# Banded attention blocks on 192 keys: a shared middle of 128 keys and two corners of 64 in a two-layer trunk on one core

## The chip, the core and the metric

One core of one Trainium2 chip runs the whole program; nothing is shared with another core. The metric is device time in microseconds (us) from start to end of one execution, lower is better. Five engines each take their own instructions in order: PE (TensorE, matrix products into PSUM; its weight loads are listed as PEld), DVE (VectorE), ACT (ScalarE), POOL (GpSimd) and SP (SyncE, which here only issues DMAs). They meet through semaphores.

## What is computed

Two layers with a residual stream of 1024 tokens by 1024 channels, all float32. The first is a gated short convolution, the second a dilated sliding-window attention with three groups of 16 heads of 64. Cut to what matters here:

```python
DILATED_GROUPS = ((128, 1), (512, 4), (2048, 16))
...
    proj = h @ w_in
    b_gate, c_gate, u, z = jnp.split(proj, 4, axis=-1)
    v = c_gate * u
    conv = sum(w_conv[k] * vp[:, k:k + S] for k in range(CONV_K))
    y = b_gate * conv * jax.nn.silu(z)
...
    logits = jnp.einsum('brhnqd,brhnkd->brhnqk', qs, kb).astype(jnp.float32) * (HEAD_DIM ** -0.5)
    step = BLOCK + a - kk
    valid = (step >= 0) & (step <= span) & (key_pos >= 0)
    logits = jnp.where(valid, logits + bias, -jnp.inf)
    probs = jnp.exp(logits - lse[..., None])
    out = jnp.einsum('brhnqk,brhnkd->brhnqd', probs.astype(v.dtype), vb)
```

In all three groups the window is 128 steps of the dilated sequence. A block of 128 queries therefore sees its own 128 keys and the 128 before them; the query at place a of the block needs the 129 keys from place a of the earlier block to place a of its own. The first 64 queries never need the second 64 keys of their own block, and the last 64 queries never need the first 64 keys of the earlier one: each half needs 192 of the 256. In group 0 the sequence is whole (8 blocks), in group 1 it falls into 4 residue classes (2 blocks each), in group 2 into 16 classes of 64 tokens, which have no earlier block.

## The kernel before

**Four stages.** The convolution's input products (up to some 630 us), its output products (to some 815 us), the attention's projections (to some 1590 us), and the attention itself with the output projection. The large products are split into high and low parts of type fp32r, three matmuls of 512 columns for each product; from pair to pair of weight blocks they go by Strassen's scheme (7 products of 12 matmuls in place of 8). `pair` and `strassen` (L310, L430) do that. At the start of the first stage, however, the channel blocks 0 and 1 are done plainly (L421: four weights, two halves each, 24 matmuls a product), while `mixed` (L190) prepares the sums of blocks of x (`T`) that Strassen's scheme needs, a quarter at each `next(mix)`.

**Attention.** A unit is one pair of heads (hp, 8 of them) and one group (g, 3). Its work is cut into steps: 4 for g = 0 and g = 1 with two blocks each, 2 for g = 2; 80 steps in all. `make` (L895) returns the parts of a step:

- A (L899): scores. q against k of both heads (s = 0 on partitions 0 to 63, s = 1 on 64 to 127) into a PSUM bank for each head. A block with an earlier block is here called wide, one without is called alone. A wide block takes four matmuls of 64 queries by 192 keys (L929), an alone one two of 128 by 128 (L924). DVE then adds the bias tile `bt`, negates, and takes the row's minimum (L942) into `xs`.
- E (L946): ACT's exponential of `xs` with the row's sum (L948).
- B (L950): PE transposes `xs` in pieces of 128 by 128 (L955) into a PSUM tile `pt`, and `copy` (L863) moves it to `pts`: for s = 0 on DVE in the first 22 steps (afterwards in every second step), otherwise on ACT.
- C (L959): the second product, values as weights against `pts`, into a PSUM tile `po` of 64 values by 512 queries for each head, one tile for each half of the sequence. `finish` (L983) copies a half to SBUF as soon as its last block is done. The 64 columns of one block's values stand 8 floats apart in the tile `V` (`[P, P, 8]`, key by value by block).

A wide block has two pieces of 128 keys in B and C, an alone one has one.

**What sets the order.** All five engines follow the order in which the program is written in this stage. The loop at L1228 runs over iterations k; in each it first emits A of step k, then C of step k-4 (`LC`), later pieces of older units (scaling, gate, splits), then B of step k-2 (`LB`), then E of step k, and in the end six matmuls of the output projection (`dense`, L1145) from iteration 36 on. SP loads q and k six steps ahead, the bias tiles with them, and V two steps ahead of a unit (its C comes four steps after its A). PSUM: three banks for scores, two for `pt`, two for `po`, one for `pd` of the output projection.

Of the kernel before, what the change touches and what calls it, by code (L numbers as in the profile page):

```python
# [19 lines left out]
P = 128  # L20
# [15 lines left out]
def trunk(ctx: ExitStack, tc: tile.TileContext, a, out):  # L36
# [92 lines left out]
    with tc.tile_pool(name="wq", bufs=1) as wq, tc.tile_pool(name="sle", bufs=1) as sle, \  # L129
# [199 lines left out]
        with tc.tile_pool(name="rp", bufs=1, side="right") as rp, tc.tile_pool(name="cp", bufs=2, side="right") as cp, \  # L329
# [490 lines left out]
    with tc.tile_pool(name="sp", bufs=1, space=PSUM) as sp, tc.tile_pool(name="ptp", bufs=2, space=PSUM) as ptp, \  # L820
# [11 lines left out]
        QK, VS, SZ, y2, part, ml = {}, {}, {}, {}, {}, {}  # L832
# [37 lines left out]
        def attention(hp, g):  # L870
# [4 lines left out]
            def prefetch():  # L875
                bt = []
                sk, w = ((sk0, 384), (sk1, 384), (sk2, 256))[g]
                for s in range(2):
# [5 lines left out]
                    else:  # L884
                        nc.sync.dma_start(b0, rows[:, :256])
# [9 lines left out]
            def make(js, first):  # L895

                c, xs, pts, exps = [], [], [], []

                def A():  # L899
# [6 lines left out]
                    for n, j in enumerate(js) if g == 2 else ():  # L906
# [6 lines left out]
                        if n % 2 == 0:  # L913
                            c.append((n // 2, j, 2 * j, True, True))
                    for n, j in enumerate(js) if g < 2 else ():
                        alone = j == 0 if g == 0 else j < 4
                        x0, nk = 2 * n, 1 if alone else 2
                        b = 2 * (j % 4) + j // 4 if g == 1 else j
                        vb = [b] if alone else [b - 1, b]
                        kv = slice(vb[0] * P, (b + 1) * P)  # L920
                        for s, hs in enumerate((lo, up)):
                            out_ = ps[s][:, x0:x0 + nk].rearrange("p a b -> p (a b)")
                            if alone:
                                nc.tensor.matmul(out_, q[hs, b * P:(b + 1) * P], k[hs, kv], start=True, stop=True)  # L924
                        if not alone:

                            for h in range(2):
                                for s, hs in enumerate((lo, up)):
                                    nc.tensor.matmul(ps[s][64 * h:64 * h + 64, x0:x0 + 2].rearrange("p a b -> p (a b)")  # L929
                                                     [:, 64 * h:64 * h + 192],  # L930
                                                     q[hs, b * P + 64 * h:b * P + 64 * h + 64],
                                                     k[hs, kv.start + 64 * h:kv.start + 64 * h + 192],
                                                     start=True, stop=True)
                        todo.append((slice(x0 * P, (x0 + nk) * P), j, slice(0 if nk == 2 else 128, 256)))
                        c.extend((x0 + i, j, vb[i], i == 0, i == nk - 1) for i in range(nk))
                    for s in range(2):
                        xs.append(ap.tile([P, 4, P], F32, name="xs", tag="xs", bufs=6))
# [11 lines left out]

                def B():  # L950
                    n = len(c)
                    for s in range(2):
                        pt = ptp.tile([P, 4, P], F32, name="pt", tag="pt")
                        for i in range(n):
                            nc.tensor.transpose(pt[:, i], xs[s][:, c[i][0]], ident)  # L955
                        pts.append(ap.tile([P, 4, P], F32, name="pts", tag="pts", bufs=6))
                        copy(pts[s][:, :n], pt[:, :n], s)

                def C():  # L959
                    for q in ((0, 1) if g == 2 else (js[0] // 4,)):  # L960
                        if js[0] == 0 or (g < 2 and js[0] == 4):
                            u["po", q] = opp.tile([P, HALF], F32, name="po", tag="po")
                    V = VS[hp, g]
                    for i, (x, j, vb, f, l) in enumerate(c):
                        for a in range(2) if g == 2 else ():
# [372 lines left out]
```

## Time and profile before

| | |
|---|---|
| median of 3 runs | 1924.93 us (1924.89 to 1928.53) |
| the profiled execution | 1926.97 us, its span 1925.2 us |
| PE busy over the span | 1893.9 us (98%), 10702 matmul records |
| DVE, ACT, POOL busy | 1480.2, 878.4, 901.0 us |
| HBM read and written | 192.53 and 67.64 MB |

The span is what the profiler saw of one execution; 1.8 us of the execution lie outside it. A matmul's record carries the partitions of its weights by their columns (`64*64`), then weights' and output's form. A float32 matmul leaves two records, a float32 transpose one, an fp32r matmul one. Matmuls on different parts of the array run beside each other, so the sum of their durations is more than the time they take; what a group takes is read from the starts in the timeline.

### The profile page before, as it was taken

How to read it: one execution, taken by the hardware profiler on the slowest of the kernel's cores; microseconds unless marked ns; L12 is line 12 of the kernel's file. 1: busy time of each engine (PE TensorE's matmuls, PEld its weight loads, DVE VectorE, ACT ScalarE, POOL GpSimd, SP SyncE). 2: the span in 40 equal slices, each digit the busy share in tenths (PEclk: the TensorE clock that was granted, in tenths of full speed). 3: DMA queues.
4: the chain of work that ended last, by engine and by line, in shares of the span. 5: the costliest groups of instructions: out<-in, count | busy, mean ns of one | idle time of the engine just before them, and what ended most of it. 6: DMA issues, size and time to landing. Idle time of an engine off the chain costs nothing.

```text
span 1925.2 us, 30180 instructions
## 1 busy us (share of the span) xinstructions
PE 1893.9 (98%) x10702; PEld 1549.7 (80%) x10702; DVE 1480.2 (77%) x2798; ACT 878.4 (46%) x2007; POOL 901.0 (47%) x835
## 2 busy tenths in 40 slices
PE   8999999999999999999999999999999998989999
PEld 6888888888888788888888888888888887767777
DVE  6966666666666746698898689869888877988896
ACT  6433333333333534454334443443344428867780
POOL 0356676766666211334545554555454551433240
PEclk9999999999999999999999999999999999989999
DMA  5312223222222656423323332333233338897842
GB/s 192 125 63 80 99 72 109 86 90 83 87 82 84 229 179 220 154 83 131 110 104 110 115 110 97 117 115 110 92 106 118 102 131 274 261 275 220 235 134 88
DMA packets 117800, 253.78 MB, mean 132 GB/s; under 512 B 18494, under 2 KB 23838, under 8 KB 117648
## 3 DMA queue, kind: packets, MB, share of 16 engines
q1 hardware_dynamic: 93280, 176.89, 28.4%
q0 software_dynamic: 24368, 74.95, 12.3%
q8 instruction: 84, 1.38, 0.3%
q14 instruction: 68, 0.56, 0.1%
HBM read 192.53 MB, written 67.64 MB: 135 GB/s over the span
## 4 chain that ended last, share of the span: by engine, by line
PE 89%; DMA 4%; DVE 3%; issue 2%; POOL 1%; ACT 1%; SPq 0%; DVEq 0%; POOLq 0%; ACTq 0%
PE pp L295 22%; PE pp L297 21%; PE pp L298 21%; PE pp L547 3%; PE pp L548 3%; PE pp L546 3%; PE po L976 2%; DMA nld<-nl 2%; PE pt L955 2%; PE pp L368 1%; PE pp L369 1%; PE pp L370 1%; PE ps L929 1%; PE pd L1150 1%; PE pd L1152 1%
## 5 line engine op out<-in xcount | busy, mean ns | idle before, releaser
L159 DVE TENSOR_TENSOR ws<-wr,ws 128x512 fp32r<-128x512 f32 x284 | 293.6, 1035 | 115.9 <-ACT ws L158 114.3
L158 ACT ACTIVATE ws<-wr 128x512 fp32r<-128x512 f32 x284 | 178.3, 630 | 368.3 <-PE pp L298 244.3
L158 ACT ACTIVATE ws<-sr 128x512 fp32r<-128x512 f32 x272 | 171.0, 631 | 349.6 <-PE pp L298 292.2
L159 DVE TENSOR_TENSOR ws<-sr,ws 128x512 fp32r<-128x512 f32 x272 | 226.4, 838 | 82.7 <-ACT ws L158 80.7
L270 POOL TENSOR_TENSOR sr<-wr 128x512 f32<-128x512 f32 x136 | 192.2, 1413 | 198.7 <-DMA wr<-in_conv_w_in 66.5
L307 DVE TENSOR_TENSOR f<-pp,f 128x512 f32<-128x512 f32 x204 | 139.6, 684 | 88.5 <-PE pp L298 81.3
L948 ACT ACTIVATE xs<-xs,nl 128x256 f32<-128x256 f32 (+2 forms) x384 | 160.5, 423 | 0.3 <-DVE nl L942 0.3
L303 ACT ACTIVATE f<-pp 128x512 f32<-128x512 f32 x228 | 132.3, 580 | 9.6 <-PE pp L298 9.6
L270 POOL TENSOR_TENSOR sr<-wr,sr 128x512 f32<-128x512 f32 x68 | 88.9, 1307 | 75.2 <-issue 54.1
L942 DVE CUSTOM_DVE_ANT_0 xs<-ps,bt 128x256 f32<-128x256 f32 (+2 forms) x384 | 102.9, 325 | 13.2 <-PE ps L929 6.9
L295 PE MATMUL pp<-blkf,ws 128*128 128x512 f32 x272 | 108.2, 398 | 0.7 <-ACT f L303 0.7
L295 PE MATMUL pp<-blka,ws 128*128 128x512 f32 x272 | 105.9, 389 | 0.7 <-ACT f L303 0.7
L297 PE MATMUL pp<-blkd,ws 128*128 128x512 f32 x272 | 106.3, 391 | 0.0
L295 PE MATMUL pp<-blkd,ws 128*128 128x512 f32 x272 | 106.2, 390 | 0.0
L295 PE MATMUL pp<-blkb,ws 128*128 128x512 f32 x272 | 106.2, 390 | 0.0
L298 PE MATMUL pp<-blkf,ws 128*128 128x512 f32 x272 | 106.1, 390 | 0.0
L297 PE MATMUL pp<-blkf,ws 128*128 128x512 f32 x272 | 106.1, 390 | 0.0
L298 PE MATMUL pp<-blke,ws 128*128 128x512 f32 x272 | 106.0, 390 | 0.0
L295 PE MATMUL pp<-blke,ws 128*128 128x512 f32 x272 | 105.9, 389 | 0.0
L295 PE MATMUL pp<-blkg,ws 128*128 128x512 f32 x272 | 105.9, 389 | 0.0
L298 PE MATMUL pp<-blkb,ws 128*128 128x512 f32 x272 | 105.8, 389 | 0.0
L297 PE MATMUL pp<-blkb,ws 128*128 128x512 f32 x272 | 105.8, 389 | 0.0
(339 smaller groups left out, 5202.1 us busy)
## 6 DMA issues: line engine op xcount, KB each, us to landing
wr<-in_conv_w_in SPq DMA_DIRECT2D x128, 256.0 KB, 3.1
wr<-in_wqk SPq DMA_DIRECT2D x96, 256.0 KB, 3.3
qkd<-blkc POOLq DMA_DIRECT2D x48, 512.0 KB, 3.9
qk<-qkd SPq DMA_DIRECT2D x48, 512.0 KB, 5.5
wr<-in_conv_w_out SPq DMA_DIRECT2D x64, 256.0 KB, 3.2
f<-in_x SPq DMA_DIRECT2D x48, 256.0 KB, 4.6
wr<-in_wv SPq DMA_DIRECT2D x48, 256.0 KB, 3.2
vd<-blkc POOLq DMA_DIRECT2D x96, 128.0 KB, 2.8
```

What stands on the lines that cost most here:

```text
L158: nc.scalar.activation(t[:, 0], src, AF.Copy)
L159: nc.vector.tensor_tensor(t[:, 1], src, t[:, 0].bitcast(F32), op=OP.subtract)
L270: nc.gpsimd.tensor_tensor(t, x, y, op=op)
L295: nc.tensor.matmul(ps, w[:, 0, ws], b[:, k, 0], start=new and k == 0, stop=False, skip_group_check=not new)
L297: nc.tensor.matmul(ps, w[:, 0, ws], b[:, k, 1], start=False, stop=False, skip_group_check=not new)
L298: nc.tensor.matmul(ps, w[:, 1, ws], b[:, k, 0], start=False, stop=end and k == 3, skip_group_check=not new)
L303: nc.scalar.activation(t, ps, AF.Copy)
L307: nc.vector.tensor_tensor(m, ps, m, op=OP.add)
L546: nc.tensor.matmul(ps[dt], w[:, 0, ws], b[:, k, 0], start=(q == k == 0), stop=False)
L547: nc.tensor.matmul(ps[dt], w[:, 0, ws], b[:, k, 1], start=False, stop=False)
L942: nc.vector.tensor_tensor_reduce(out=x, in0=flat[s][:, cols], in1=u["bt"][s][:, bs], op0=OP.add, op1=OP.min, scale=-1.0, scalar=3e38, accu ...
L948: nc.scalar.activation(x, x, AF.Exp, bias=nm, scale=-1.0, accum_out=L)
```

## The change

In the attention a wide block now works on 192 columns of scores in place of 256. Columns 64 to 191 are the shared middle: keys -64 to 63 of the block, for all 128 queries. Columns 0 to 63 are a corner: for the first 64 queries keys -128 to -65, for the last 64 queries keys 64 to 127. So A has three matmuls for each head (192, 128 and 64 keys), and bias, exponential and `pts` copy run over 192 columns a block. The middle is transposed by one 128 by 128 transpose; each corner by a 64 by 64 matmul against the identity, four of them (two heads, two halves) in the four quarters of the array (`corners`, emitted right behind A, for the step whose B comes in the same iteration). In the second product a corner is a 64 by 64 by 64 matmul, again four in four quarters. The middle needs values that straddle two blocks: a new tile `W` holds V shifted by 64 tokens, loaded by two more DMAs for each unit with g < 2. `po` is now one tile for each half of the 64 queries within a block (not for each half of the sequence), so the middle's and the alone blocks' second products run for each half by itself, 64 columns at a time, and both `po` tiles of a unit are finished together at its end. The bias tile is loaded in three pieces.

In the convolution's first stage, of channel block 1 only the weights 0 and 1 are done plainly; the other two become the first pair of Strassen's scheme, and `T` is prepared correspondingly earlier.

```diff
-            for k in range(4):
+            for k in range(2):
                 plain_w(1, k, 2)
-                if k < 3:
+                next(mix)
+                if k == 0:
                     next(mix)
                 for hf in range(2):
                     evac(1, k, hf, products(k, hf))
-
-            pairs = [(e, pr) for e in range(2, NE) for pr in range(2)]
+                    if k:
+                        taps(1, hf)
+
+            pairs = [(e, pr) for e in range(1, NE) for pr in range(2)][1:]
...
+            if g < 2:
+                t = WS[hp, g] = ap.tile([P, P + 1, 8], F32, name="W", tag="W", bufs=2)
+                t = t.rearrange("p a b -> p (a b)")
+                nc.sync.dma_start(t[:64, 1:S + 1], vd[hp, g, 64:])
+                nc.sync.dma_start(t[64:, :S], vd[hp, g, :64])
...
-                        nc.sync.dma_start(b0, rows[:, :256])
+                        nc.sync.dma_start(b0[lo], rows[:64, :256])
+                        nc.sync.dma_start(b0[up, 64:], rows[64:128, 64:256])
+                        nc.sync.dma_start(b0[up, :64], rows[64:128, 192:256])
...
+                            for h, to, at_, m in ((0, 0, -P, 192), (1, 64, -64, P), (1, 0, 64, 64)):
                                 for s, hs in enumerate((lo, up)):
+                                    nc.tensor.matmul(flat[s][64 * h:64 * h + 64, x0 + to:x0 + to + m],
                                                      q[hs, b * P + 64 * h:b * P + 64 * h + 64],
+                                                     k[hs, b * P + at_:b * P + at_ + m], start=True, stop=True)
...
+                def corners():
...
+                            for h, hs in enumerate((lo, up)):
+                                for s in range(2):
+                                    x = xs[s].rearrange("p a b -> p (a b)")
+                                    to = (lo, up)[h ^ s]
+                                    nc.tensor.matmul(pt[s].rearrange("p a b -> p (a b)")
+                                                     [to, 256 + 64 * n:256 + 64 * n + 64],
+                                                     x[hs, x0:x0 + 64], ident[hs, hs], start=True, stop=True)
...
-                            nc.tensor.matmul(po[:, j % 4], V[:, hs, vb], pts[s][:, i], start=f, stop=l)
...
+                                for h in range(2):
+                                    for s, hs in enumerate((lo, up)):
+                                        rs = (lo, up)[h ^ s]
+                                        p = pts[s].rearrange("p a b -> p (a b)")[rs, n:n + 64]
+                                        if s:
+                                            b0 = 512 + b + (1 if h else -1)
+                                            put(h, s, hs, j, w[rs, b0:b0 + 505:8], p)
+                                        else:
+                                            put(h, s, hs, j, V[rs, hs, b - 1 + h], p)
...
+                            for h in range(2):
+                                for s, hs in enumerate((lo, up)):
+                                    put(h, s, hs, j, (V if alone else WS[hp, g])[:, hs, b],
+                                        pts[s][:, i, 64 * h:64 * h + 64])
...
+                if lag == 0 and LB <= k < len(steps) + LB:
+                    for f in steps[k - LB].get("corners", ()):
+                        f()
```

Three places show what the engines now find in their queues. First PE, in the steady part of a unit of group 1 that follows group 0. `ps` are scores, `pt` transposed pieces, `po` the second product. Before, two iterations:

```order
L924 MATMUL ps<-qk 128x128 x4
L976 MATMUL po<-pts,V 64x128 x8
L955 MATMUL pt<-ident,xs 128x128 x8
L929 MATMUL ps<-qk 64x192 x8
L976 MATMUL po<-pts,V 64x128 x8
L955 MATMUL pt<-ident,xs 128x128 x4
```

And the first of them now:

```order
L932 MATMUL ps<-qk 128x128 x4
L970 MATMUL pt<-ident,xs 64x64 x8
L1008 MATMUL po<-pts,V 64x64
L1008 MATMUL po<-pts,W 64x64
L1008 MATMUL po<-pts,V 64x64
L1008 MATMUL po<-pts,W 64x64
L1008 MATMUL po<-pts,V 64x64
L1008 MATMUL po<-pts,W 64x64
L1008 MATMUL po<-pts,V 64x64
L1008 MATMUL po<-pts,W 64x64 x9
L983 MATMUL pt<-ident,xs 128x128 x4
```

Of the eight transposes four are left; eight corner matmuls stand ahead of the second product, and that has 16 matmuls of 64 columns where it had 8 of 128.

Second SP, the loads from one group 1 to the next group 2 (`sk` are bias rows, `qkd` and `vd` the stored projections). Before:

```order
L885 DMA bt<-sk_85 128x256 x2
L838 DMA qk<-qkd 128x1024 x2
L847 DMA V<-vd 128x512 x2
L56 DMA wraw<-in_wo 128x1024 x2
L883 DMA bt<-sk_86 64x64 x4
```

Now:

```order
L893 DMA bt<-sk_85 64x256
L894 DMA bt<-sk_85 64x192
L895 DMA bt<-sk_85 64x64
L893 DMA bt<-sk_85 64x256
L894 DMA bt<-sk_85 64x192
L895 DMA bt<-sk_85 64x64
L841 DMA qk<-qkd 128x1024 x2
L850 DMA V<-vd 128x512 x2
L855 DMA W<-vd 64x1024
L856 DMA W<-vd 64x1024
```

Two DMAs more for `W` behind V, and six for the bias where there were two.

Third DVE, the end of a unit (`o<-po` is `finish`, `pts<-pt` the copy of B). Before, half of the unit's output is copied at its second step and half, as here, at its last:

```order
L942 ISA xs,nl<-ps,bt 128x256
L942 ISA nl 128x1
L991 COPY o<-po 128x512
L866 COPY pts<-pt 128x256
L942 ISA xs,nl<-ps,bt 128x256
L942 ISA nl 128x1
```

Now both copies stand together at the last step:

```order
L950 ISA xs,nl<-ps,bt 128x192
L950 ISA nl 128x1
L1045 COPY o<-po 128x2x256 x2
L874 COPY pts<-pt 128x256
L950 ISA xs,nl<-ps,bt 128x192
L950 ISA nl 128x1
```

The copy of the middle of the unit has moved to its end, and the bias operation is 192 wide.

More of the change, by code (lines that the diff above doesn't have):

```diff
@@ L830, in parts_tile @@
             return t
-        QK, VS, SZ, y2, part, ml = {}, {}, {}, {}, {}, {}
+        QK, VS, WS, SZ, y2, part, ml = {}, {}, {}, {}, {}, {}, {}
         acc = [ap.tile([P, S], F32, name="acc", tag=f"acc{dt}", bufs=1) for dt in range(KT)]
@@ L895, in make @@
             def make(js, first):
-                c, xs, pts, exps = [], [], [], []
+                c, xs, pts, exps, pt = [], [], [], [], []
                 def A():
@@ L914, in A @@
                             c.append((n // 2, j, 2 * j, True, True))
+                    x0 = 0
                     for n, j in enumerate(js) if g < 2 else ():
                         alone = j == 0 if g == 0 else j < 4
-                        x0, nk = 2 * n, 1 if alone else 2
                         b = 2 * (j % 4) + j // 4 if g == 1 else j
[L919 to L924, printed above, removed]
@@ L925, in A @@
-                        if not alone:
-                            for h in range(2):
+                        w = P if alone else 192
+                        if alone:
+                            for s, hs in enumerate((lo, up)):
+                                nc.tensor.matmul(flat[s][:, x0:x0 + P], q[hs, b * P:(b + 1) * P],
+                                                 k[hs, b * P:(b + 1) * P], start=True, stop=True)
+                        else:
+                            for h, to, at_, m in ((0, 0, -P, 192), (1, 64, -64, P), (1, 0, 64, 64)):
@@ L934, in A @@
-                        todo.append((slice(x0 * P, (x0 + nk) * P), j, slice(0 if nk == 2 else 128, 256)))
-                        c.extend((x0 + i, j, vb[i], i == 0, i == nk - 1) for i in range(nk))
+                                                     k[hs, b * P + at_:b * P + at_ + m], start=True, stop=True)
+                        todo.append((slice(x0, x0 + w), j, slice(128, 256) if alone else slice(0, 192)))
+                        c.append((x0, j, b, alone))
+                        x0 += w
@@ L950, in B @@
                 def B():
-                    n = len(c)
+                    n = len(c) * P + sum(64 for x in c if g < 2 and not x[3])
                     for s in range(2):
[L953 to L957, printed above, removed]
+                        x = xs[s].rearrange("p a b -> p (a b)")
+                        if g == 2:
+                            pt.append(ptp.tile([P, 4, P], F32, name="pt", tag="pt"))
+                        for i in range(len(c)):
+                            x0 = i * P if g == 2 else c[i][0] + (0 if c[i][3] else 64)
+                            nc.tensor.transpose(pt[s][:, i], x[:, x0:x0 + P], ident)
+                        pts.append(ap.tile([P, 3, P], F32, name="pts", tag="pts", bufs=6))
+                        copy(*(y.rearrange("p a b -> p (a b)")[:, :n] for y in (pts[s], pt[s])), s)
@@ L959, in C @@
                 def C():
[L960 to L961 removed]
+                    V = VS[hp, g]
+                    if js[0] == 0:
+                        for q in range(2):
                             u["po", q] = opp.tile([P, HALF], F32, name="po", tag="po")
[L963 to L976 removed]
@@ L979, in C @@
+                    if js[-1] == 7:
+                        for q in range(2):
                             finish(q)
-                return [A, B, C, E]
+                return [A, B, C, E, corners]
             def finish(q):
@@ L1110, in attention @@
                     st = make(js, not steps)
-                    steps.append({lag: [f] for lag, f in zip((0, LB, LC, "exps"), st)})
+                    steps.append({lag: [f] for lag, f in zip((0, LB, LC, "exps", "corners"), st)})
             end = steps[-1]
```

53 lines of the change are left out of this document (36 added, 17 removed).

## The prediction

> **What bounds the kernel now.** First the chain that ended last, then the attention stage by stretches (columns: length; busy time of PE, PEld, DVE, ACT, POOL; granted PE clock, DMA share, GB/s), then the waits in it.
>
> ```profile
> PE 89%; DMA 4%; DVE 3%; issue 2%; POOL 1%; ACT 1%; SPq 0%; DVEq 0%; POOLq 0%; ACTq 0%
> 1593.00:1700.00 107.00, 97.96 (x1390) 78.57 (x1391) 93.04 (x434) 95.06 (x386) 33.04 (x43) 0.95 0.87 277
> 1700.00:1885.00 185.00, 177.81 (x2145) 140.84 (x2143) 163.59 (x600) 132.96 (x518) 62.54 (x77) 0.98 0.67 199
> PE pt L955 <- DVE pts L866: 5.5, 6, 2.1
> PE po L976 <- DVE o L988: 5.1, 5, 1.4
> PE pd L1150 <- DVE acc L1186: 4.1, 1, 4.1
> PE ps L924 <- DMA qk<-qkd: 1.5, 1, 1.5
> ```
>
> PE is busy for 276 of the 292 us; what it waits for is 15 us of DVE's and 3 at the start. Up to 1700 us DVE and ACT are nearly as full; later PE alone is. So an us more on PE is close to an us more in all, and relief of DVE and ACT can at best give back those 15 us and what follows on a wait: a lower granted clock.
>
> ```profile
> 1660.00:1670.00 10.00, 9.09 (x80) 7.21 (x84) 8.89 (x38) 7.40 (x23) 4.40 (x8) 0.66 0.71 229
> 1690.00:1700.00 10.00, 9.21 (x90) 7.69 (x91) 9.53 (x37) 7.56 (x29) 2.72 (x4) 0.83 0.97 281
> 1720.00:1730.00 10.00, 5.94 (x63) 4.27 (x61) 8.81 (x21) 4.42 (x18) 4.81 (x4) 0.76 0.82 288
> 1730.00:1740.00 10.00, 10.00 (x111) 8.09 (x112) 9.32 (x28) 7.41 (x22) 4.81 (x8) 0.89 0.61 192
> ```
>
> Busy time times the missing clock is 3.1 + 1.6 + 1.4 + 1.1 = 7 us lost.
>
> **The change on PE.** The counts come from these rows, a matmul counting twice, a transpose once:
>
> ```profile
> L955 PE MATMUL pt<-ident,xs 128*128 128x128 f32 x496 | 75.7, 289 | 5.6 <-DVE pts L866 5.5
> L976 PE MATMUL po<-pts,V 128*64 128x128 f32 x864 | 71.1, 303 | 5.1 <-DVE o L988 5.1
> L929 PE MATMUL ps<-qk 64*64 64x192 f32 x704 | 41.3, 342 | 1.1 <-DVE nl L942 1.1
> L924 PE MATMUL ps<-qk 64*128 64x128 f32 x160 | 16.7, 313 | 1.5 <-DMA qk<-qkd 1.5
> ```
>
> 704 / 8 = 88 wide blocks, 160 / 4 = 40 alone. Durations overlap, so paces come from starts in the timeline (start, duration, what, records):
>
> ```profile
> 1671.63 0.66 PE L955 MATMUL pt<-ident,xs 128*128 128x128 f32 x4
> 1672.21 0.69 PE L910 MATMUL ps<-qk 64*64 64x64 f32 x32
> 1672.84 0.76 PE L976 MATMUL po<-pts,V 128*64 128x128 f32 x8
> 1673.53 1.09 PE L955 MATMUL pt<-ident,xs 128*128 128x128 f32 x8
> 1674.55 0.69 PE L910 MATMUL ps<-qk 64*64 64x64 f32 x32
> ...
> 1712.59 0.49 PE L924 MATMUL ps<-qk 64*128 64x128 f32 x4
> 1713.01 0.56 PE L929 MATMUL ps<-qk 64*64 64x192 f32 x8
> 1713.50 1.24 PE L976 MATMUL po<-pts,V 128*64 128x128 f32 x16
> 1714.67 0.66 PE L955 MATMUL pt<-ident,xs 128*128 128x128 f32 x4
> ...
> 1721.30 1.08 PE L969 MATMUL po<-pts,V 64*64 64x64 f32 x32
> 1722.31 0.88 PE L955 MATMUL pt<-ident,xs 128*128 128x128 f32 x6
> ```
>
> L976 takes 1.17 us for 16 records and 0.69 for 8: 0.48 for four pairs, **0.12 a pair**, and 0.21 once for the change of array shape. L955: 1.02 for 8, 0.58 for 4, so 0.11 each and 0.15 once. In the four quarters, L910's eight rounds of four take 0.63, or 0.48 less a change of shape: 0.06 to 0.08 a round. L969, also 64 by 64 by 64, takes 1.01 for eight rounds: 0.11 to 0.126. What differs is the weights, not the size:
>
> ```profile
> L976 PEld LDWEIGHTS po<-pts,V 128*64 128x64 f32 x864 | 58.4, 211 | 17.4 <-issue 9.1 <-DVE o L988 6.0
> L929 PEld LDWEIGHTS ps<-qk 64*64 64x64 f32 x704 | 23.3, 135 | 14.1 <-issue 10.2 <-DVE nl L942 2.0
> L969 PEld LDWEIGHTS po<-pts,V 64*64 64x64 f32 x512 | 18.2, 210 | 1.3 <-DVE o L991 0.6 <-issue 0.4
> ```
>
> 64 weight columns that lie together (q) load in 135 ns; V's, 8 floats apart, in 211, on four quarters and on two halves alike. I read a pair of L976 as bound by this load, not by its 128 columns: L969 streams only 64 and takes as long. The change halves the columns that follow each such load and doubles the loads. Then:
>
> - Second product. Wide: four pairs (0.48) become two corner rounds (0.24) and four middle pairs (0.48 by the load): +0.24 x 88 = **+21.1**. Alone: two pairs become four: +0.24 x 40 = **+9.6**. The trace has no pair with 64 columns and spread weights. Bounds: L910's 0.06 a round throughout (wide -0.12, alone 0: -10.6) and L969's 0.126 (wide +0.276, alone +0.264: +34.8). I take 0.12, because both rows that load V lie there.
> - Transposes. Wide: two fewer, -0.22; two corner rounds with contiguous weights, +0.13 (0.065 each): -0.09 x 88 = **-7.9** (+2.8 at L969's pace).
> - Scores. The same 192 columns for each quarter, but two of the four get them in two matmuls. Nothing if the quarters run freely; if the 64 columns stand behind the rest, two rounds of 0.06: +10.6. I take 0.03 a block, **+2.6**, near the free end, since a round of 192 (0.16 by L929) leaves room.
> - Shape changes. In 16 steps (the first two of a group 1 unit) the corners stand behind 64 by 128 scores, not 64 by 64 ones: one change more, 0.1 to 0.2: **+2.4**.
>
> PE's sum: 21.1 + 9.6 - 7.9 + 2.6 + 2.4 = **+27.8** (from -18 to +51 with all bounds at one end).
>
> On the weight step: in the Trainium skill, "SBUF — State Buffer", section "Specifications (TRN2)" gives lines of 16 bytes, of which at least two hits are needed for full bandwidth; V's and W's columns lie 32 bytes apart. By that rule the narrow pairs pay as the wide ones and the sum stands; without it, it is the first rival's. The trace agrees as far as it goes (211 against 135 ns).
>
> **Relief on DVE and ACT.**
>
> ```profile
> L942 DVE CUSTOM_DVE_ANT_0 xs<-ps,bt 128x256 f32<-128x256 f32 x176 | 64.9, 419 | 6.7 <-PE ps L929 4.4 <-ACT xs L948 1.6
> L942 DVE CUSTOM_DVE_ANT_0 xs<-ps,bt 128x128 f32<-128x128 f32 x80 | 19.3, 286 | 4.4 <-PE ps L929 2.5 <-ACT xs L948 1.4 <-PE ps L924 0.5
> L866 DVE COPY pts<-pt 128x512 f32<-128x512 f32 x23 | 15.7, 684 | 0.6 <-PE pt L955 0.6
> ...
> L948 ACT ACTIVATE xs<-xs,nl 128x256 f32<-128x256 f32 x176 | 87.1, 500 | 0.3 <-DVE nl L942 0.3
> L948 ACT ACTIVATE xs<-xs,nl 128x128 f32<-128x128 f32 x80 | 31.1, 393 | 0.0
> ```
>
> Halfway between its rows a bias operation of 192 columns takes 353 ns and an exponential 447: 176 x 66 = 11.6 us off DVE, 176 x 53 = 9.3 off ACT; a quarter less in the 512-wide copies, some 100 ns x 23, adds 2.3 on DVE, and on ACT likewise. These lie beside PE; on the path they count only through the 15 + 7 us above. Two things work against that. Corners need `pt`, so the copy of the step before must be done 1.17 us (C's length) sooner than now: behind it on PE's queue stand C, B and all else. And a unit of group 0 or 1 frees both `po` tiles only at its end, as group 2 does now, which is where the 5.1 us of waits for L988 arise; two copies in a row then have only B, A and corners to hide behind. So I count a third of the 22 us as gained: **-7.5** (0 to -22).
>
> **Loads.** 32 DMAs of 256 KB for W, 8.4 MB, and 64 more bias issues stand on SP's queue, ahead of the next unit's loads. They are issued six steps, over 14 us, ahead of use; V's issues at the same place landed within 12.6 us at worst:
>
> ```profile
> DMA to landing us min/median/max: 2.6/5.9/12.6
> ...
> 80.00:90.00 10.00, 10.00 (x46) 8.28 (x45) 10.00 (x16) 3.94 (x8) 1.72 (x1) 1.00 0.11 40
> 450.00:500.00 50.00, 50.00 (x223) 41.39 (x222) 30.47 (x34) 17.81 (x31) 35.74 (x28) 1.00 0.25 80
> ```
>
> **+0.5** for the first unit, which has only four steps; 0 to +10.
>
> **The first stage.** 96 matmuls become 84: 12 x 50 / 223 = -2.7. But `T` is wanted 22 us sooner, and DVE, which makes it, is full there (80 to 90 us). I take **-2** (-2.7 to +4).
>
> Sum against the profiled execution: 1926.97 + 27.8 - 7.5 + 0.5 - 2 = 1945.8. That execution lies 2.0 us above the median of the runs, so against these I say **1944**, slower.
>
> **The rivals.**
>
> 1. Faster: narrow pairs load as contiguous weights do. Place: each middle pair; it decides below about 0.08 us a pair. At 0.06 throughout, PE changes by -10.6 - 7.9 + 2.6 + 2.4 = -13.5; two thirds of the 22 us come back: -15 - 2 + 0.5; 1895. For it: 64 columns stream in half of 128's time. Against: L969. Chance 0.08.
> 2. No change: PE's rise is real but lets DVE catch up everywhere: all 22 us regained, scores and shapes free: 27.8 - 5 - 22 - 2 + 0.5 = -0.7; 1924. For it: DVE has less to do in a longer stage. Against: the two earlier needs. Chance 0.10.
> 3. A new wait: PE at the corners for DVE's copy. About four steps in ten hold a DVE operation of over 1 us ahead of it; 14 of the 35 steps up to 1700 us losing up to 1.17 us give up to 16, half taken, and nothing regained: 27.8 + 8 - 2 + 0.5; 1959. Chance 0.13.
> 4. Transfers: up to 1700 us the DMAs are 87% busy, and 3.5 head pairs add 3.7 MB, 13 us at 277 GB/s. PE's own rise hides most; where it doesn't, +8: 1952. Chance 0.06.
> 5. Quarters in turn: corners of both row halves write one PSUM bank, which no row here does (L910 and L969 keep a bank for each row half). If they alternate, 176 rounds of transposes take 0.065 more: +11; 1955. Chance 0.05. The Trainium skill, "TensorEngine Tiling (Array Packing)", section "Gotcha 1: PSUM Pressure", says that different row tiles cannot access the same PSUM bank simultaneously; the sum with it is this rival's, without it the forecast's. No row here tests it.
>
> That the change does not do what it says shows in no place: the order of PE has the corners and halves as described.
>
> **How the numbers follow.** The forecast has 0.58 with its own 1930 to 1958. From 1925 (half of the second rival below it) to 1962 (a tenth above, when scores, corners and copies all go the wrong way) the range leaves out two in ten. A change of 0.2%, 3.9 us, is about what a measurement of this kernel can tell from none. Faster: rival 1, 0.08. Same: rival 2, 0.10. Slower: 0.58 + 0.13 + 0.06 + 0.05 = 0.82.
>
> **What would show it.** The second product's weight loads near 211 ns, and starts 0.12 us apart for its narrow pairs; a step with two wide blocks in A, B and C 0.3 us longer than its 3 us; PE still busy over 92% of the stage. It is wrong if these pairs stand 0.06 to 0.08 apart, if PE's waits for `pts` and `o` grow beyond 15 us, or if the corners' rounds come two by two.

## The result, and the profile after

| | time (us) | against the kernel before |
|---|---|---|
| before | 1926.73 median of 4 (1924.89 to 1929.39) | |
| after | 1960.28 median of 4 (1959.96 to 1965.37) | 1.0178 [1.0162, 1.0193] |
| the profiled execution of after | 1960.56, span 1958.8 | |

The change makes the kernel 33.6 us slower. The prediction said slower, by 19 us. As in the prediction, a pair is two records side by side on two halves of the array, and a round four records in its four quarters.

First the chain that ended last, of the kernel after.

```profile
PE 86%; DVE 3%; DMA 3%; issue 2%; POOL 1%; ACT 1%; SPq 0%; DVEq 0%; POOLq 0%; ACTq 0%
PE pp L295 21%; PE pp L297 21%; PE pp L298 21%; PE po L1008 4%; PE pp L550 3%; PE pp L551 3%; PE pp L549 3%; PE pt L983 2%; PE ps L938 1%; DMA nld<-nl 1%; PE pd L1205 1%; PE pd L1207 1%; PE pd L1206 1%; PE pt L970 1%; PE ps L932 0%
```

The second product was L976 with 2% in the chain and is now L1008 with 4%. All other large shares belong to stages that the change hardly touches. So the place to look at is the attention stage. Its first score starts at 1592.97 us before and at 1592.34 after; its last second product ends at 1882.5 and 1915.7. The stage is some 34 us longer, which is the whole difference. Here it is as one stretch, first of before and then of after (length; busy time of PE, PEld, DVE, ACT, POOL; PE clock, DMA share, GB/s).

```profile
1593.00:1883.00 290.00, 273.77 (x3506) 217.45 (x3506) 254.73 (x1030) 228.01 (x903) 95.58 (x120) 0.97 0.75 230
```

```profile
1593.00:1916.00 323.00, 299.50 (x5240) 253.11 (x5232) 238.89 (x1030) 212.81 (x903) 95.03 (x119) 0.96 0.84 232
```

Length less PE's busy time is idle time. PE is busy 25.7 us longer and idle 23.5 us in place of 16.2, 7.3 more. DVE and ACT have 16 and 15 us less work, as the change intends, and PE waits longer all the same. The DMAs are busier in a longer stage: 0.75 x 290 = 218 us before, 0.84 x 323 = 271 after.

What PE does longer is read from two steps late in the stage that nothing disturbs. Timeline of PE, before (start, duration, what, records; the output projection's matmuls left out):

```profile
1815.66 0.72 PE L924 MATMUL ps<-qk 64*128 64x128 f32 x8
1816.31 1.24 PE L976 MATMUL po<-pts,V 128*64 128x128 f32 x16
1817.48 1.09 PE L955 MATMUL pt<-ident,xs 128*128 128x128 f32 x8
1819.90 0.88 PE L929 MATMUL ps<-qk 64*64 64x192 f32 x16
1820.71 1.24 PE L976 MATMUL po<-pts,V 128*64 128x128 f32 x16
1821.88 0.66 PE L955 MATMUL pt<-ident,xs 128*128 128x128 f32 x4
```

The same two steps after:

```profile
1842.51 0.71 PE L932 MATMUL ps<-qk 64*128 64x128 f32 x8
1843.15 0.46 PE L970 MATMUL pt<-ident,xs 64*64 64x64 f32 x16
1843.43 0.28 PE L1008 MATMUL po<-pts,V 64*64 64x64 f32 x1
...
1844.03 1.19 PE L1008 MATMUL po<-pts,W 128*64 128x64 f32 x16
1845.14 0.66 PE L983 MATMUL pt<-ident,xs 128*128 128x128 f32 x4
1847.12 0.90 PE L938 MATMUL ps<-qk 64*64 64x192 f32 x24
1847.82 0.26 PE L1008 MATMUL po<-pts,V 64*64 64x64 f32 x2
...
1849.54 0.66 PE L983 MATMUL pt<-ident,xs 128*128 128x128 f32 x4
```

For two wide blocks the second product took 1.17 us (1816.31 to 1817.48) and takes 1.71 (1843.43 to 1845.14): +0.27 a block. Corner and middle transposes, up to the next step's scores (six matmuls of the output projection among them, before and after), took 2.42 and take 0.28 + 1.98: -0.08 a block. The scores took 0.81 and take 0.70: -0.055 a block. A likely reason is that the change of array shape that stood behind them now stands inside the second product; it was not tested. The eight middle pairs alone take 1.11 us, as the eight wide pairs took 1.17 with twice the columns. Two alone blocks took 0.70 us (1792.51 to 1793.21) and take 1.11 (1860.70 to 1861.81): +0.205 a block. Over 88 wide and 40 alone blocks these rows make some 20 us.

The waits are where the forecast missed most. PE's waits in the stage, after (total, times, longest):

```profile
PE pt L970 <- DVE pts L874: 13.4, 8, 3.1
PE po L1008 <- DMA W<-vd: 3.0, 1, 3.0
PE ps L932 <- DMA qk<-qkd: 2.1, 2, 1.8
PE pd L1205 <- DVE acc L1241: 1.8, 1, 1.8
PE pt L970 <- ACT xs L956: 1.2, 4, 0.4
```

L955's 5.5 us behind DVE's copy became L970's 13.4. L976's 5.1 us behind `o` are gone, although both `po` tiles are now freed together. W brings a wait of its own. DVE's timeline at the longest of L970's waits shows how the copy gets late there:

```profile
1702.12 0.08 DVE L950 DVE_READ_ACCUMULATOR2_ANT nl<- 128x1 f32 x1
1704.81 0.18 DVE L1070 TENSOR_TENSOR mx<-ml 128x16 f32<-128x16 f32 x1 [2.62 <-DMA ml<-nld]
...
1705.43 1.22 DVE L1100 TENSOR_TENSOR o<-o,sqacc 128x1024 f32<-128x1024 f32 x1
1706.56 0.48 DVE L874 COPY pts<-pt 128x320 f32<-128x320 f32 x1
```

DVE stands still for 2.6 us, waiting for an 8 KB load of row statistics of an older unit; behind that come the merge of two groups, 1.2 us, and only then the copy for which PE waits with the corners. It is the only one of the eight waits in which DVE is seen to stand still for a load. In the other large ones (1.95 us up to 1638.04, 2.66 up to 1674.78, 1.45 up to 1794.23, 1.73 up to 1876.47) the copy stands behind DVE's own work on older units: one operation of 1.2 us, two copies of `o` of 1.9 us together or both, and short operations on the row statistics. The clock goes with such a wait (stretches of 10 us, columns as above):

```profile
1673.00:1683.00 10.00, 8.22 (x142) 7.09 (x142) 7.57 (x30) 6.81 (x21) 3.36 (x5) 0.66 0.88 247
1703.00:1713.00 10.00, 6.19 (x106) 5.27 (x106) 7.20 (x24) 4.19 (x17) 3.73 (x4) 0.66 0.88 246
```

Over all such stretches of the stage, busy time times the missing clock (below: the lost clock) adds up to 6.5 us before and 9.0 after. Busy time less lost clock is below called work: of the 25.7 us that PE is busy longer some 23 are work. Idle time and lost clock together are 22.7 us before and 32.5 after.

### The profile page after: what moved, and what is told of

It reads as the page before. It is cut to its first block, busy times and chain, and to the rows that moved or that the text cites. A ratio compares the mean times of both kernels' runs of the same rounds, so it can differ in the third digit from the quotient of the medians.

```text
span 1958.8 us, 33817 instructions
## 1 busy us (share of the span) xinstructions
PE 1919.8 (98%) x12434; PEld 1584.7 (81%) x12434; DVE 1464.6 (75%) x2802; ACT 864.4 (44%) x2013; POOL 910.1 (46%) x841
## 4 chain that ended last, share of the span: by engine, by line
PE 86%; DVE 3%; DMA 3%; issue 2%; POOL 1%; ACT 1%; SPq 0%; DVEq 0%; POOLq 0%; ACTq 0%
PE pp L295 21%; PE pp L297 21%; PE pp L298 21%; PE po L1008 4%; PE pp L550 3%; PE pp L551 3%; PE pp L549 3%; PE pt L983 2%; PE ps L938 1%; DMA nld<-nl 1%; PE pd L1205 1%; PE pd L1207 1%; PE pd L1206 1%; PE pt L970 1%; PE ps L932 0%
## 5 line engine op out<-in xcount | busy, mean ns | idle before, releaser
L159 DVE TENSOR_TENSOR ws<-wr,ws 128x512 fp32r<-128x512 f32 x283 | 282.0, 998 | 118.2 <-ACT ws L158 117.3
L270 POOL TENSOR_TENSOR sr<-wr 128x512 f32<-128x512 f32 x138 | 197.3, 1430 | 254.6 <-DMA wr<-in_conv_w_in 113.4
L159 DVE TENSOR_TENSOR ws<-sr,ws 128x512 fp32r<-128x512 f32 x276 | 234.6, 856 | 86.1 <-ACT ws L158 83.9
L956 ACT ACTIVATE xs<-xs,nl 128x192 f32<-128x192 f32 (+2 forms) x384 | 151.0, 398 | 0.3 <-DVE nl L950 0.3
L950 DVE CUSTOM_DVE_ANT_0 xs<-ps,bt 128x192 f32<-128x192 f32 (+2 forms) x384 | 91.0, 295 | 26.7 <-PE ps L938 13.3
L295 PE MATMUL pp<-blkf,ws 128*128 128x512 f32 x276 | 109.8, 398 | 0.7 <-ACT f L303 0.7
L295 PE MATMUL pp<-blke,ws 128*128 128x512 f32 x276 | 107.7, 390 | 0.2 <-ACT f L303 0.2
L295 PE MATMUL pp<-blkb,ws 128*128 128x512 f32 x276 | 107.7, 390 | 0.0
L298 PE MATMUL pp<-blkf,ws 128*128 128x512 f32 x276 | 107.7, 390 | 0.0
L297 PE MATMUL pp<-blkf,ws 128*128 128x512 f32 x276 | 107.6, 390 | 0.0
L298 PE MATMUL pp<-blke,ws 128*128 128x512 f32 x276 | 107.6, 390 | 0.0
L298 PE MATMUL pp<-blkb,ws 128*128 128x512 f32 x276 | 107.4, 389 | 0.0
L297 PE MATMUL pp<-blke,ws 128*128 128x512 f32 x276 | 107.4, 389 | 0.0
```

The costliest lines, as they stand in the source:

```text
L159: nc.vector.tensor_tensor(t[:, 1], src, t[:, 0].bitcast(F32), op=OP.subtract)
L270: nc.gpsimd.tensor_tensor(t, x, y, op=op)
L295: nc.tensor.matmul(ps, w[:, 0, ws], b[:, k, 0], start=new and k == 0, stop=False, skip_group_check=not new)
L297: nc.tensor.matmul(ps, w[:, 0, ws], b[:, k, 1], start=False, stop=False, skip_group_check=not new)
L298: nc.tensor.matmul(ps, w[:, 1, ws], b[:, k, 0], start=False, stop=end and k == 3, skip_group_check=not new)
L950: nc.vector.tensor_tensor_reduce(out=x, in0=flat[s][:, cols], in1=u["bt"][s][:, bs], op0=OP.add, op1=OP.min, scale=-1.0, scalar=3e38, accu ...
```

## The experiments

The theory at the outset: the time grew by PE's second product, which loads spread weights twice as often; and the relief of DVE and ACT did not come, because the corners want the copies earlier. The first half stands after the experiments, the second only in part. The rivals: W's loads; quarters in turn because of a shared bank; another cause for the pace of narrow pairs. All ratios are to the kernel before, run on the same chip.

**The second product by itself.** In the kernel before:

```diff
-                            nc.tensor.matmul(po[:, j % 4], V[:, hs, vb], pts[s][:, i], start=f, stop=l)
+                            for h in (lo, up):
+                                nc.tensor.matmul(po[:, j % 4, h], V[:, hs, vb], pts[s][:, i, h],
+                                                 start=(i == 0 and js[0] % 4 == 0 and h == lo), stop=True,
+                                                 skip_group_check=True)
```

> The kernel before, with each matmul of the second product of groups 0 and 1 split into two of 64 columns, as the change does; nothing else. If a narrow pair is bound by its spread weight load (0.12 us a pair, as wide ones): 432 pairs become 864, PE has 432 x 0.12 = 52 us more, some of it in place of DVE's waits (15 us): 1965 to 1980 us, starts of narrow pairs 0.12 us apart. Rival, bound by the columns: pairs 0.06 apart, no more PE time: 1920 to 1932 us.

Measured: 1967.58 us, 1.0217 [1.0198, 1.0236], +42.5 us and in the range of the first case. The group of its weight loads, and the second product of two wide blocks:

```profile
L977 PEld LDWEIGHTS po<-pts,V 128*64 128x64 f32 x1728 | 112.3, 214 | 14.8 <-issue 9.1 <-DVE o L991 3.4
1821.29 2.19 PE L977 MATMUL po<-pts,V 128*64 128x64 f32 x32
1823.40 0.66 PE L955 MATMUL pt<-ident,xs 128*128 128x128 f32 x4
```

Its attention stage (columns as for the stage above):

```profile
1593.00:1921.00 328.00, 317.91 (x4340) 267.17 (x4343) 253.56 (x1029) 229.07 (x903) 95.51 (x120) 0.99 0.65 203
```

A pair of half the columns costs as much as a whole one: 16 pairs take 2.11 us where 8 took 1.17. Of the 52 us of added work some 10 were regained: PE is idle 10.1 us in place of 16.2, and the lowest clock of the 10 us stretches is 0.91 where it was 0.66 (1.6 us lost in place of 6.5). So where PE alone gets slower, part of the waits goes; the forecast's cover exists to that extent. The lost clock of a single profile says little by itself: `before_act` below, which adds no work on PE, lost 1.5 us.

**Neighbouring weights.** In the kernel after, all weights of the second product are read through `near` (the second helper, 2 apart, in a kernel of its own); the same in the kernel before. In all three the second product takes other values than it should.

```diff
+        def near(t, rows, s, b):
+            return t.rearrange("p a b -> p (a b)")[rows, 512 * s + 64 * b:512 * s + 64 * b + 64]
...
-                                            put(h, s, hs, j, V[rs, hs, b - 1 + h], p)
+                                            put(h, s, hs, j, near(V, rs, s, b - 1 + h), p)
...
```

```diff
+        def near(t, rows, s, b):
+            b0 = 512 * s + 128 * (b // 2) + b % 2
+            return t.rearrange("p a b -> p (a b)")[rows, b0:b0 + 127:2]
...
```

> The changed kernel, but the 64 weight columns of a block's values are read from 64 neighbouring floats of the tiles V and W and not from 64 floats that stand 8 apart, so the second product takes other values than it should; loads, counts and order are the same. If the spread of the weights sets the pace: weight loads of the second product fall from 211 to about 135 ns, rounds from 0.12 to about 0.06 us; 528 rounds and pairs of wide blocks, 160 of alone ones and 64 of group 2 save up to 752 x 0.06 = 45 us of PE, part of which comes back as waits for DVE: 1915 to 1940 us. Rival, the pace of narrow pairs has another cause (columns, issue of four instructions): 1955 to 1962 us.

> The changed kernel with the weight columns 2 floats apart (other values than it should). If two floats of one 16-byte line are enough for a full-pace load: as with neighbouring floats, within 4 us of that kernel. If the load time grows with the distance itself: about a quarter of the way or more back to 1960 us, weight loads of 145 ns or more.

> The kernel before with the same addressing by neighbouring floats (other values than it should). If a wide pair of 128 columns is bound by its weights alone, 432 pairs save 0.05 us each and group 2 four us: 1900 us or less. If its 128 columns take as long as the spread load (0.10 to 0.11 us as in the alone blocks' scores): 432 x 0.01 and group 2's 4 us: 1916 to 1924 us.

Measured: after with neighbouring floats 1947.66 us, 1.0113 [1.0089, 1.0136]; 2 floats apart 1948.22 us, 1.0107 [1.008, 1.0133]; before with neighbouring floats 1923.41 us, 0.9989 [0.9978, 1.0]. Of after with neighbouring floats, first the group of weight loads of the middle pairs (count, busy time, mean ns):

```profile
L1011 PEld LDWEIGHTS po<-pts,W 128*64 128x64 f32 x704 | 26.1, 145 | 2.8
```

PE's timeline, the second product of two wide blocks up to the transposes:

```profile
1814.08 0.22 PE L1011 MATMUL po<-pts,V 64*64 64x64 f32 x2
...
1815.05 0.65 PE L986 MATMUL pt<-ident,xs 128*128 128x128 f32 x4
```

The largest waits of its PE:

```profile
PE pt L973 <- DVE pts L874: 18.0, 11, 4.7
PE ps L941 <- issue: 9.3, 6, 3.3
PE ps L923 <- issue: 4.5, 3, 2.2
```

Its attention stage:

```profile
1593.00:1904.00 311.00, 263.04 (x5205) 211.53 (x5207) 234.41 (x1029) 214.05 (x903) 95.16 (x120) 0.93 0.88 241
```

The same weight loads where the floats are 2 apart:

```profile
L1012 PEld LDWEIGHTS po<-pts,W 128*64 128x64 f32 x704 | 25.7, 141 | 2.8
```

The weights set the pace: the second product of two wide blocks takes 0.97 us in place of 1.72 (1847.82 to 1849.54 above), 0.06 us less in each of its 12 rounds. Two floats in 16 bytes are enough: 141 and 145 ns against 211 with one. In the Trainium skill, "SBUF — State Buffer", section "Specifications (TRN2)" asks for at least two hits on a 16-byte line; the trace agrees. But of the 43 us of PE work that this saves in the stage (290 to 247 us) only 12.6 reach the time, which lies between the ranges of the expectation's two cases. PE is now busy 10.7 us less than in the kernel before (273.77), at a clock of 0.93, and idle 48 us: the stage is bound by what it waits for.

The kernel before stays in the range that was expected for its 128 columns, but its trace says more than that. Its second product of two wide blocks, and its stage:

```profile
1822.50 1.09 PE L979 MATMUL po<-pts,V 128*64 128x128 f32 x16
1823.52 0.66 PE L958 MATMUL pt<-ident,xs 128*128 128x128 f32 x4
1593.00:1883.00 290.00, 267.24 (x3488) 204.30 (x3488) 251.09 (x1030) 227.73 (x903) 96.45 (x120) 0.94 0.76 231
```

The wide pairs do get faster, 1.02 us in place of 1.17, and PE's work in the stage falls by some 15 us, from 267 to 252. Idle time and lost clock take it back: 22.8 and 15.5 us in place of 16.2 and 6.5. This profile is the slowest of its ten executions, 4.2 us above their median, but that median too lies only 1.65 us [0 to 4.2] below the kernel before.

**The corners later.** In the kernel after:

```diff
-                if lag == 0 and LB <= k < len(steps) + LB:
+                if lag == LB and LB <= k < len(steps) + LB:
                     for f in steps[k - LB].get("corners", ()):
                         f()
+                for f in steps[k - lag].get(lag, ()) if 0 <= k - lag < len(steps) else ():
+                    f()
```

(The last two lines stood ahead of it.)

> The changed kernel with the corner transposes emitted right ahead of B's transposes, behind C, and not behind A. If the early need of the corners turns DVE's late copies into waits of PE (13.4 us at the corners in the profile): those waits fall to the 5 us that the kernel before had at L955, and the granted clock loses 1 to 2 us less; against it stands one more change of array shape in the 48 steps with wide blocks, 0.15 to 0.2 us each, 7 to 10 us: 1955 to 1962 us, with the waits for pts below 6 us. Rival, the copies are late however early they are wanted: the waits stay at 12 us or more and the time rises to 1966 us or more.

Measured: 1965.24 us, 1.0211 [1.0186, 1.0236]. PE's largest waits in the stage:

```profile
PE pt L970 <- DVE pts L874: 7.1, 6, 4.7
PE ps L938 <- issue: 3.8, 3, 1.5
```

The waits for copies fall by half, to 7.1, of which 4.7 are one wait on the small load; so with the early need go some 6 us of waits for copies. But the kernel does not get faster: both the time and the waits lie between the numbers of the two cases. Idle time falls to 18.5 us, the lost clock rises to 17 from 9, and shapes change once more in a step. So that the early need makes the kernel slower is not shown by this.

**All copies on ACT.** In the kernel after:

```diff
-            if s == 0 and (flip[0] % 4 == 1 or flip[0] < 44):
+            if False:
```

> The changed kernel with every copy of pt on ACT, none on DVE (25 us of busy time moves). If PE waits at the corners because the copy of head 0 stands in DVE's queue behind merges and normalisations of older units: the 13.4 us of waits for DVE's copies go, 10 us or more of them for good, and some clock with them: 1944 to 1952 us. Rival, ACT is as late (its exponentials stand ahead of the copy): waits for ACT's copies of 8 us or more in their place, 1956 to 1966 us.

Measured: 1957.73 us, 1.0169 [1.0148, 1.0191], not to be told from the change itself. PE's largest waits in the stage:

```profile
PE pd L1205 <- DVE acc L1241: 4.1, 1, 4.1
PE ps L932 <- DVE nl L950: 3.9, 2, 3.7
...
PE pt L970 <- ACT pts L876: 1.6, 2, 1.2
```

Neither case's numbers: the copies are hardly waited for on either engine (1.6 us), and the time stays within 3 us. Idle time and lost clock are 16.8 and 13.9 us, together 30.7 where the changed kernel has 32.5. The stop at 1702 us, where DVE waits for a small load, is still there; PE now meets it at the scores (3.7) and another at the output projection (4.1), behind the other things in DVE's queue. Taking the copy out of the queue moves the wait. So it is not the wait at the corners as such that costs the time.

**A bank for each row half.** In the kernel after:

```diff
-                                    nc.tensor.matmul(pt[s].rearrange("p a b -> p (a b)")
+                                    nc.tensor.matmul(pt[h].rearrange("p a b -> p (a b)")
...
-                                        p = pts[s].rearrange("p a b -> p (a b)")[rs, n:n + 64]
+                                        p = pts[h].rearrange("p a b -> p (a b)")[rs, n:n + 64]
```

> The changed kernel with the corners of the first query half written to one PSUM bank and those of the second half to the other, so that no bank is written by two row halves of the array (before: one bank for each head). Same result and counts. If quarters that share a bank run in turn, 176 rounds get 0.06 us shorter: 1948 to 1951 us. If not: 1958 to 1963 us and rounds of corners as far apart as they are.

Measured: 1959.95 us, 1.0184 [1.0165, 1.0204]: no change. The rows of after above say the same: eight corner transposes, 16 records in four rounds, take 0.28 us (1843.15 to 1843.43), 0.07 a round, though two row halves write one bank in each (on different partitions of it); here they take as long (1838.86 to 1839.14). The Trainium skill, "TensorEngine Tiling (Array Packing)", section "Gotcha 1: PSUM Pressure", says that different row tiles cannot access the same PSUM bank simultaneously; for these transposes it costs nothing that shows.

**Without W.** In the kernel after; middles and corners then read V, so that the second product takes other values than it should.

```diff
-                t = WS[hp, g] = ap.tile([P, P + 1, 8], F32, name="W", tag="W", bufs=2)
-                t = t.rearrange("p a b -> p (a b)")
-                nc.sync.dma_start(t[:64, 1:S + 1], vd[hp, g, 64:])
-                nc.sync.dma_start(t[64:, :S], vd[hp, g, :64])
+                WS[hp, g] = VS[hp, g]
...
```

> The changed kernel without the 32 loads of W: middles and corners read V in its place, so that the second product takes other values than it should. If the loads cost no more than the 3.0 us of PE's wait for W and the clock behind it, and part of the 3.4 us stop at 1704 us where DVE waits for a small load: 1953 to 1958 us. Rival, the full DMA queues hold more than that (up to 1720 us the DMAs are at 87% and over): 1948 us or less.

Measured: 1953.76 us, 1.0153 [1.0135, 1.0172], 6.5 us below after. The stage:

```profile
1593.00:1909.00 316.00, 296.79 (x5215) 251.95 (x5214) 239.41 (x1027) 212.57 (x902) 94.80 (x119) 0.97 0.72 210
```

The DMAs' busy time falls from 271 to 0.72 x 316 = 228 us. So W's 8.4 MB take 43 us of the DMAs, not the 27 that they would at the 230 GB/s and 0.75 of before (307 GB/s at a full share). They cost 6.5 us in the end; the time lies in the first case's range, near its lower edge. PE's wait for W and DVE's stop of 2.6 us are gone, and idle time falls from 23.5 to 19.2 us (the lost clock is 8.7, from 9.0); the waits for copies at the corners stay (14.6 us), so W's loads do not make them.

**The relief by itself.** In the kernel before, bias and exponential of a wide block leave out its first 64 columns (their old numbers stay; the tiles `xs` are kept and zeroed once on POOL):

```diff
-                        todo.append((slice(x0 * P, (x0 + nk) * P), j, slice(0 if nk == 2 else 128, 256)))
+                        todo.append((slice(x0 * P + 64 * (nk - 1), (x0 + nk) * P), j,
+                                     slice(64 if nk == 2 else 128, 256)))
...
-                        xs.append(ap.tile([P, 4, P], F32, name="xs", tag="xs", bufs=6))
+                        xs.append(XS[turn_x[0] % 6])
```

> The kernel before, in which the bias operation and the exponential of a wide block leave out its first 64 columns (they keep old numbers, so the output is not the reference's): 11.6 us less on DVE and 9.3 on ACT, as in the change, and nothing else. If relief of DVE and ACT by itself gives back PE's waits for copies and some clock: 1916 to 1922 us, the 10.6 us of waits for pts and o down to 6 or less. Rival, the waits hang on the long merges and small loads that stand in DVE's queue, not on its load: 1923 to 1927 us, waits as they were. By the first, the changed kernel lost its relief to the earlier need of the corners and to W; by the second there was none to lose.

Measured: 1926.74 us, 1.0001 [0.9993, 1.001]. The largest waits:

```profile
PE pt L961 <- DVE pts L870: 4.5, 5, 1.5
PE po L982 <- DVE o L994: 4.1, 3, 2.6
```

8.6 us for copies and `o`, where the kernel before has 10.6; another wait, for DVE's row minimum, is 3.0 in place of 1.1. Some 23 us less work in the stage, 14 on DVE and 9 on ACT, are worth nothing that can be measured (the interval is -1.3 to +1.9 us). The kernel before with all copies on ACT gives the same answer:

> The kernel before with every copy of pt on ACT, none on DVE. If DVE's queue is what makes the copies late there too: 5.5 us of waits for DVE's copies and some of the 5.1 for o go, 1916 to 1922 us. Rival, ACT is up to 1700 us as full as DVE (95 of 107 us busy), and the copies wait behind exponentials: 1925 to 1935 us.

Measured: 1926.01 us, 1.0 [0.9991, 1.0009]. PE waits 4.4 us for ACT's copies where it waited 5.5 for DVE's, and 5.5 for `o`.

**The convolution's part alone**, in the kernel before; its diff is the first block of the change's.

> The kernel before with the convolution's part of the change alone. By the prediction 12 matmuls less, 2.7 us, of which DVE's full queue takes some: 1922 to 1925 us. By the trace of the changed kernel, whose attention starts 0.7 us earlier: 1924 to 1926 us. Rival, DVE's earlier sums cost more than the matmuls: 1927 us or more.

Measured: 1922.62 us, 0.998 [0.9971, 0.9989]. This part makes the kernel 3.6 us faster (2.1 to 5.6 by the interval, so the 2.7 of its 12 matmuls lie within). Its attention starts at 1589.99 us, against 1592.97 before; single executions of the unchanged part differ by some half a us either way (1592.29 and 1593.43 in the two kernels above). In the profile of the whole change the attention starts only 0.6 us sooner. It is the only version here that computes the right output and is clearly below both kernels.

**Neighbouring weights and copies on ACT together**, in the kernel after (again with other values).

> The changed kernel with both: neighbouring weight columns (so the second product takes other values than it should) and all copies of pt on ACT. By the runs before, PE's work in the attention stage is then some 12 us below that of the kernel before. If the copies in DVE's queue were all that kept the time at 1947 us: the 18 us of waits at the corners go with their clock, 1920 to 1928 us. If the waits hang on the long operations and small loads in DVE's queue whichever wait comes first: they turn up at the scores and second products, waits and clock loss together stay above 35 us, 1935 to 1945 us.

Measured: 1943.8 us, 1.0095 [1.0069, 1.0121], in the range of the second case. The largest waits of PE:

```profile
PE pd L1207 <- DVE acc L1243: 6.9, 3, 5.4
PE ps L935 <- DVE nl L953: 5.1, 3, 4.5
PE ps L941 <- issue: 4.8, 3, 3.5
PE pt L973 <- issue: 4.3, 3, 2.1
```

And the stage:

```profile
1593.00:1896.00 303.00, 265.77 (x5225) 214.70 (x5226) 215.06 (x979) 227.90 (x954) 95.08 (x119) 0.92 0.89 247
```

PE has 8 us less busy time than before, at a lower clock (18 us lost), and DVE 40 us less, but PE is idle for 37 us, and the stage is 13 us longer. The waits are spread over scores, transposes, second products and the output projection. What is high is the DMAs' share, 0.89: 0.89 x 303 = 270 us of transfers, which the kernel before, at 218, did not have. That these are now the bound would fit, and the 6.5 us without W point that way; a kernel with neighbouring weights and without W was not run, so it stays open how much of the 37 us are theirs. What the waits named "issue" are is open too. The chain that ended last, asked for this stage alone, names another candidate: 10.5% of it are transfers `nld<-nl`, with which POOL stores the row statistics, and 4.4% their loads `ml<-nld`, more than any line of PE has. In the kernel before they have 13.0% and 2.6% of the chain; in the split, where PE's added work reaches the time, neither is among the lines named. No run shortened this path, so what it costs is not shown.

## Why the prediction was right, and where it was not

The direction was right, and 1960 lies in the stated range, 2 us below its end. It lies outside the forecast's own 1930 to 1958, 16 us above 1944: the change costs 33.6 us where 19 were said. PE's part was right in mechanism and near in size; the relief and the loads were not. Of the signs that were named, the weight loads (208 to 215 ns), the step (0.27 us longer for two wide blocks) and PE's busy share (92.7%) came as said; the waits for `pts` and `o`, 14.5 us, stayed just below the 15 that would have spoken against it.

- **What bounds the kernel.** Right for added work on PE: 42.5 of 52 us reached the time in the split. Not right for saved work: with neighbouring weights in the kernel before, some 15 us less work gave 1.65. More work on PE lengthens the stage nearly in full, less work runs into its other waits; the prediction did not price the two apart.
- **Second product, +21.1 and +9.6.** Right in mechanism, near in size: +0.27 a wide block where +0.24 was said and +0.205 an alone one for 0.24, 23.8 and 8.2 us. The pace falls with the load time when the weights stand together. Rival 1 fell with it.
- **Transposes, -0.09 a block.** Right (-0.08). Rival 5 fell: no rounds in turn.
- **Scores +2.6 and shape changes +2.4.** Wrong in sign: the wide scores got 0.055 us shorter a block, -4.8 us over 88 blocks, of which the second product's 0.03 a block may take some back. With this the rows add up to 20 us of work, and the stage shows 23, where 27.8 were said.
- **Relief, -7.5.** This is the step that failed. In its place stand 7.3 us more of idle time and 2.5 more of lost clock. Less work on DVE and ACT was worth nothing: the relief alone gave 0.0. The waits that were looked at hang on what stands ahead of the awaited copy in DVE's queue, not on how full the queue is over the stage. The earlier need of the corners does show in the waits, 13.4 us at L970 where L955 had 5.5, but it is not shown to be what the 10 us are: with the corners later these waits halved, with the copies on ACT they nearly went, and the time did not fall with them. So its price in rival 3, whose end of 1959 us is so near, was met partly by luck. Freeing both `po` tiles together cost little: there is no wait for `o` at L1008 among the larger ones, though in one wait at the corners (1.13 us up to 1665.45) the awaited copy stands behind the two copies of `o`.
- **Loads, +0.5.** Mis-sized: 6.5 us, near rival 4's +8. This is part of the 10 us above and not on top of them: without W, idle time and lost clock are 27.9 us in place of 32.5. What the rest of the 10 us hangs on stays open.
- **The first stage, -2.** Mis-sized: -3.6 by itself (-2.1 to -5.6). In the changed kernel 0.6 us of it is seen at the start of the attention, where PE waits for q and k.
- **Rival 2, no change,** had the idea of regained time right for a slower PE, but not here.

In the stage, 23 of work, 7.3 of idle time and 2.5 of clock are 33, the difference of the two stretches. This is the same difference taken apart and no second proof of it. How it falls into idle time and clock changes from one execution to the next: the kernel with a bank for each row half, which takes the same time, has 20.5 and 10.5 us where the changed kernel has 23.5 and 9.0.

## What to carry to other kernels

Before narrowing a product, ask whether its columns or its weights set the pace: here 64 spread weight columns load in 0.21 us and 128 columns stream no slower, so half the columns saved nothing and twice the products cost double. Price an added and a saved microsecond apart: in this stage 52 us more on PE cost 42.5, and some 15 less gave 1.65. Before counting on work taken from an engine that is often waited for, look at what stands ahead of the awaited instruction in its queue: here 23 us less work was worth nothing that could be measured. And where a wait has been removed and the time stays, look for the wait that took its place before calling the first one the cause.

## What the runs showed of the hardware

- 64 float32 weight columns load in 145 ns when they stand together, in 141 at a distance of 2 floats and in 211 to 215 at 8.
- Corner transposes of 64 by 64 in the four quarters, two row halves on different partitions of one PSUM bank, take 0.07 us for each round of four records (two rounds for four transposes), and no less with banks of their own.
- The 10 us stretch that holds a wait of PE of 3.1 us (1704.06 to 1707.19) has a mean granted clock of 0.66; the one that holds a wait of 1.95 us (up to 1638.04) has 0.85.
